# Two more projections formed with seven half products, head norms scaled by ScalarE, and memory attention bridged last, in a two-layer hybrid trunk

## The chip, the cores and the metric

One core of a Trainium2 chip runs the kernel. Its engines are TensorE (matmuls), VectorE, ScalarE, GpSimd and SyncE, each with its own queue of instructions, and 16 DMA engines that move data between the chip's memory and the on-chip buffers. The metric is the device time of one execution, in microseconds (us), as the median of several runs.

## The reference

Two layers over x of shape 256 x 2048 in float32. Every layer makes one wide projection of the normed rows, cuts it into four branches (A sparse attention, B retention, C a gated recurrence, M attention into 256 memory tokens), gates each branch, projects it, weighs it with a sigmoid gate and adds all four. Cut to what matters here:

```python
def hybrid_layer(x, mem, norm_g, w_in, qk_g, ret_g, hgrn_g, lb, w_mem_kv, w_branch, w_out, cos, sin):
    h = rms_norm(x, norm_g)
    u = h @ w_in                                   # 2048 x 15944
    (a_q, a_k, a_v, a_z, a_qi, a_ki, a_wi, b_q, b_k, b_v, b_z,
     c_f, c_i, c_q, c_z, m_q, m_z, gates) = split_cols(u)
    y_a = sparse_index_attention(head_rms_norm(a_q), head_rms_norm(a_k), a_v, a_qi, a_ki, a_wi)
    y_b = head_rms_norm(retention(rope(b_q), rope(b_k) * HEAD_DIM ** -0.5, b_v), ret_g)
    y_c = head_rms_norm(hgrn2(lb + (1.0 - lb) * sigmoid(c_f), c_i, c_q), hgrn_g)
    mkv = mem @ w_mem_kv
    y_m = memory_attention(head_rms_norm(m_q), head_rms_norm(mkv[..., :W]), mkv[..., W:])
    for n, (y, z) in enumerate(((y_a, a_z), (y_b, b_z), (y_c, c_z), (y_m, m_z))):
        merged += sigmoid(gates[:, :, n]) * ((y * silu(z)) @ w_branch[n])
    return x + merged @ w_out
```

## The kernel before

All large products run on TensorE in the type fp32r, with both operands split into a high and a low part: three matmuls (`whi` x high, `wlo` x high, `whi` x low) stand for one. The weights come from memory in slabs of 512 rows and 512 columns (`raw`, 1 MB, four buffers). ScalarE casts a half slab to `whi`, VectorE subtracts to get `wlo` (`cut_piece`), and four pairs of `whi` and `wlo` buffers stand between them and TensorE. A plain slab has two halves, and TensorE runs 12 matmuls of 128x512 on each: two 128-row blocks of weights, times both halves of the 256 rows of x, times three (`gemms`, tiles `u`, `bw`, `wo`).

Some pairs of 512-column chunks are made as a group (`product`, tile `px`): the 256 rows and the 2048 contracted columns are taken as two by two blocks, and seven products of 128 x 1024 by 1024 x 512 stand for eight. The sums of weight blocks that these need are built in four `sum` tiles: a plain DMA from SyncE writes a block into a tile, and DMAs from GpSimd add further blocks (`accum_op`), one for each stage, each after the split that read the tile (`add_block`, `STAGES`). Product number 5 (`RING`) takes plain weights from `raw`. A half of a group's weights feeds only 6 matmuls, since only 128 rows of x (or sums of rows: `r4`, `s1` to `s3`) go with it. Outputs are added up in the tiles `qs`, `us`, `one` (`take`, `combined`). The last sum of the group "c" is made by VectorE from the `raw` tile of product 5 (`sum<-sum,raw`), that of the other groups by one more DMA (`LAST_SUM`). Before, five groups in each layer are done so: the recurrence's values and gate ("c"), and for each of the four branches two of its four gate chunks (`DUO`).

A layer has an early stage (the projections of all branches; the products of group "c" are mingled with plain slabs by `early_tokens`) and a gate stage (gates, four groups, and the bridges, that is branch outputs times `w_branch`, tile `bw`; `gate_tokens`), then the output projection (`wo`). The memory's keys and values for both layers are made first of all and parked in memory.

The program text is written by a planner: after every half of weights, `Stream.pump` lets tasks (Python generators, one for a branch's steps) put their next instructions into the engines' queues, unless a running account of each engine's work says that VectorE or ScalarE is late. `stream.ticks` counts slabs; many tasks wait for a tick (`gates_at + n`), others for a key in `box`. If a task is needed at once and not done, `finish` forces its steps out. The queues then run in the order written. Every instruction is recorded by a helper, so all compute carries line 127 or 145 and is told apart by its tiles.

## Time and profile before

| | before |
|---|---|
| runs | 1814.96, 1815.46, 1817.58 us (median 1815.46) |
| profiled execution | 1814.12 us, of it 1812.3 us from the first to the last instruction |
| TensorE busy | 1803.3 us, 8836 matmuls |
| VectorE, ScalarE, GpSimd busy | 1346.4, 1058.6, 374.4 us |
| moved by DMA | 451.45 MB |
| granted TensorE clock | 1.00 |

In the profile PE is TensorE's matmul, PEld its weight load, DVE is VectorE, ACT ScalarE, POOL GpSimd and SP SyncE. A row of a group gives the tiles written and read, the shapes, the count, the busy time and the mean duration in ns, and behind the bar the idle time of the engine before these instructions with what ended it. Layer 0's early products start at 163 us and its gate stage near 437 us; layer 1's start at 1022 and 1287 us.

### The profile page before, as it was taken

How to read it: one execution, taken by the hardware profiler on the slowest of the kernel's cores; microseconds unless marked ns; L12 is line 12 of the kernel's file. 1: busy time of each engine (PE TensorE's matmuls, PEld its weight loads, DVE VectorE, ACT ScalarE, POOL GpSimd, SP SyncE). 2: the span in 40 equal slices, each digit the busy share in tenths (PEclk: the TensorE clock that was granted, in tenths of full speed). 3: DMA queues.
4: the chain of work that ended last, by engine and by line, in shares of the span. 5: the costliest groups of instructions: out<-in, count | busy, mean ns of one | idle time of the engine just before them, and what ended most of it. 6: DMA issues, size and time to landing. Idle time of an engine off the chain costs nothing.

```text
span 1812.3 us, 24371 instructions
## 1 busy us (share of the span) xinstructions
PE 1803.3 (100%) x8836; PEld 1499.9 (83%) x8836; DVE 1346.4 (74%) x1458; ACT 1058.6 (58%) x1261; POOL 374.4 (21%) x565
## 2 busy tenths in 40 slices
PE   9999999999999999999999999999999999999999
PEld 8889888888888888888887988888888888888887
DVE  5677798786878777687665778878777877777764
ACT  4756565455667656555455656545657765655442
POOL 0022330033232111112131241103333211110200
PEclk9999999999999999999999999999999999999999
DMA  9769965789999999986795996578999999998773
GB/s 332 269 213 289 292 209 180 256 226 277 278 255 278 292 223 274 260 242 219 238 285 155 312 266 207 187 247 225 264 287 272 252 297 228 275 263 234 233 235 136
DMA packets 125321, 451.45 MB, mean 249 GB/s; under 512 B 23184, under 2 KB 45456, under 8 KB 92432
## 3 DMA queue, kind: packets, MB, share of 16 engines
q1 hardware_dynamic: 90480, 357.71, 56.9%
q0 software_dynamic: 34432, 91.92, 26.2%
q8 instruction: 69, 1.13, 0.3%
q14 instruction: 52, 0.43, 0.1%
q10 hardware_dynamic: 288, 0.26, 0.0%
HBM read 419.66 MB, written 6.29 MB: 235 GB/s over the span
## 4 chain that ended last, share of the span: by engine, by line
PE 98%; DVE 1%; DMA 1%; issue 0%; POOL 0%; ACT 0%; SPq 0%; DVEq 0%
PE u L145 50%; PE px L145 21%; PE bw L145 10%; PE wo L145 10%; PE mv L145 2%; PE mk L145 2%; PE ixrp L145 0%; PE mov L145 0%; PE mlg L145 0%; DVE wlo L127 0%; PE bo L145 0%; PE co L145 0%; PE aov L145 0%; DMA xp<-xpi 0%; PE cl L145 0%; PE bs L145 0%
## 5 line engine op out<-in xcount | busy, mean ns | idle before, releaser
L127 DVE TENSOR_TENSOR wlo<-raw,whi 128x1024 fp32r<-128x1024 f32 (+3 forms) x556 | 656.1, 1187 | 344.1 <-ACT whi L127 339.0
L127 ACT CAST whi<-raw 128x1024 fp32r<-128x1024 f32 (+3 forms) x556 | 568.2, 1025 | 581.6 <-PE u L145 352.0
L127 DVE TENSOR_TENSOR wlo<-sum,whi 128x1024 fp32r<-128x1024 f32 x240 | 288.2, 1222 | 67.4 <-ACT whi L127 60.7
L127 ACT CAST whi<-sum 128x1024 fp32r<-128x1024 f32 x240 | 250.2, 1052 | 99.9 <-PE px L145 49.8
L127 POOL DMA_DIRECT2D sum<-in_win x152 | 138.3, 919 | 620.6 <-DVE wlo L127 594.9
L145 PE MATMUL u<-whi,x12h 128*128 128x512 f32 (+2 forms) x176 | 67.4, 383 | 1.5 <-ACT x12h L127 1.5
L145 PE MATMUL u<-whi,x12l 128*128 128x512 f32 (+2 forms) x176 | 67.1, 381 | 0.5 <-DVE x12l L127 0.5
L145 PE MATMUL u<-whi,x13h 128*128 128x512 f32 (+2 forms) x176 | 67.6, 384 | 0.0
L145 PE MATMUL u<-whi,x01h 128*128 128x512 f32 (+2 forms) x176 | 67.5, 383 | 0.0
L145 PE MATMUL u<-whi,x02h 128*128 128x512 f32 (+2 forms) x176 | 67.4, 383 | 0.0
L145 PE MATMUL u<-whi,x11h 128*128 128x512 f32 (+2 forms) x176 | 67.4, 383 | 0.0
L145 PE MATMUL u<-whi,x00h 128*128 128x512 f32 (+2 forms) x176 | 67.3, 383 | 0.0
L145 PE MATMUL u<-whi,x10h 128*128 128x512 f32 (+2 forms) x176 | 67.3, 382 | 0.0
L145 PE MATMUL u<-whi,x03h 128*128 128x512 f32 (+2 forms) x176 | 67.1, 381 | 0.0
L145 PE MATMUL u<-wlo,x12h 128*128 128x512 f32 (+2 forms) x176 | 67.1, 381 | 0.0
L145 PE MATMUL u<-wlo,x13h 128*128 128x512 f32 (+2 forms) x176 | 67.1, 381 | 0.0
L145 PE MATMUL u<-wlo,x11h 128*128 128x512 f32 (+2 forms) x176 | 67.1, 381 | 0.0
L145 PE MATMUL u<-wlo,x01h 128*128 128x512 f32 (+2 forms) x176 | 67.0, 381 | 0.0
L145 PE MATMUL u<-wlo,x02h 128*128 128x512 f32 (+2 forms) x176 | 67.0, 381 | 0.0
L145 PE MATMUL u<-wlo,x10h 128*128 128x512 f32 (+2 forms) x176 | 67.0, 381 | 0.0
L145 PE MATMUL u<-wlo,x00h 128*128 128x512 f32 (+2 forms) x176 | 67.0, 381 | 0.0
L145 PE MATMUL u<-whi,x00l 128*128 128x512 f32 (+2 forms) x176 | 67.0, 381 | 0.0
(496 smaller groups left out, 4482.5 us busy)
## 6 DMA issues: line engine op xcount, KB each, us to landing
raw<-in_win SPq DMA_DIRECT2D x180, 1024.0 KB, 6.7
sum<-in_win POOLq DMA_DIRECT2D x152, 512.0 KB, 8.5
sum<-in_win SPq DMA_DIRECT2D x80, 512.0 KB, 6.9
raw<-in_wbr SPq DMA_DIRECT2D x32, 1024.0 KB, 6.8
raw<-in_wout SPq DMA_DIRECT2D x32, 1024.0 KB, 5.4
raw<-in_wmem SPq DMA_DIRECT2D x12, 1024.0 KB, 4.9
raw<-in_win SPq DMA_DIRECT2D x8, 656.0 KB, 4.3
xc<-in_x SPq DMA_DIRECT2D x8, 512.0 KB, 6.8
```

Of the source, the lines that this page charges most:

```text
L127: return call(*args, **kw)
L145: return self.engine.matmul(out, w, x, **kw)
```

## The change

- Attention's values and gate (`O_AV`, `O_AZ`) become a sixth group "a", behind "c": `EARLY_GROUPS` names the chunks, and the four `sum` tiles go on from "c" to "a" to the gates' groups without being opened anew.
- The chunks of memory attention's and retention's queries and keys (`O_MQ`, `O_MZ`, `O_BQ`, `O_BK`), which stood as plain slabs without products between the early products and the gate stage, are mingled with the products of "c" and "a".
- `scaled_rows`: the multiplication of each head's row by its inverse root (queries, keys, the two branch norms) and of the softmax rows by their inverse sums is done by ScalarE, one instruction for each head and row half, in place of one VectorE instruction.
- Memory attention starts on events (`attended`, `mq`, `mp`) in place of ticks, and the bridges run in the order C, A, B, M in place of C, A, M, B.
- `gate_path` keeps the sigmoid in the tile of its result; the general pool has 23 buffers in place of 22, and the scratch of GpSimd's DMA descriptors 2048 bytes in place of 4096.
- At the end of layer 0 the third chunk's task is stepped twice at once; `finish` lets all other tasks step; the two tables are loaded one at a time.

```diff
-BR_ORDER = (2, 0, 3, 1)
+BR_ORDER = (2, 0, 1, 3)
-GEN, HL, RAW = 22, 4, 4
-DUO, AHEAD, FIRST, MERGED = (2, 0, 3, 1), 10, 0, (0, 3, 2, 1)
-FOLLOWED = dict(zip(DUO, DUO[1:]))
+GEN, HL, RAW = 23, 4, 4
+DUO, AHEAD, FIRST, MERGED = (2, 0, 1, 3), 10, 0, (0, 3, 2, 1)
+FOLLOWED = dict(zip(("c", "a") + DUO, ("a",) + DUO))
-LAST_SUM, RING, EARLY = (True, 1, 0), 5, 8
+LAST_SUM, RING, EARLY, EARLY_GROUPS = (True, 1, 0), 5, 8, {"c": (O_CI, O_CZ), "a": (O_AV, O_AZ)}
...
             elif not moved:
-                ahead = self.tasks[:self.tasks.index(t)]
+                ahead = [u for u in self.tasks if u is not t]
...
 def early_tokens():
-    rows = [("chunk", c, n, b) for c, n in CHUNKS[4:10] for b in range(4)]
-    return rows[:EARLY] + mingled(products_of("c"), rows[EARLY:])
+    rows = [("chunk", c, n, b) for c, n in CHUNKS[4:8] + CHUNKS[10:14] for b in range(4)]
+    return rows[:EARLY] + mingled(products_of("c") + products_of("a"), rows[EARLY:])
...
+    def scaled_rows(out, src, scales, n):
+        for i in range(src.shape[1]):
+            ac.activation(out[:, i, :], src[:, i, :], AF.Copy, scale=scales[:, i:i + 1])
+            if i % n == n - 1 and i < src.shape[1] - 1:
+                yield
...
-            ve.tensor_mul(qn, qn, bc(r, HD))
+            yield from scaled_rows(qn, qn, r, 4)
...
-        ve.tensor_mul(y1, v, bc(r, HD))
+        yield from scaled_rows(y1, v, r, 4)
...
-        ve.tensor_mul(p, p, bc(rc, nk))
+        yield from scaled_rows(p, p, rc, 2)
...
-            ac.activation(sg[:, t, :], ps[:, t, :], AF.Sigmoid, scale=rs[:, t:t + 1])
-            ve.scalar_tensor_tensor(zs[:, t, :], ps[:, t, :], rs[:, t:t + 1], sg[:, t, :],
+            ac.activation(zs[:, t, :], ps[:, t, :], AF.Sigmoid, scale=rs[:, t:t + 1])
+            ve.scalar_tensor_tensor(zs[:, t, :], ps[:, t, :], rs[:, t:t + 1], zs[:, t, :],
...
-        br[0] = stream.add(attend(..., "a", gates_at + 38))
-        box[key("av")] = evac(early_slabs(O_AV), rs, "av")
-        stream.add(keep(key("az"), transposed(gate_path(early_slabs(O_AZ), rs, "az"), "azt")))
+        br[0] = stream.add(attend(..., "a", gates_at + 48, key("attended")))
+        stream.add(keep(key("mq"), put_off(key("attended"), normed_t(early_slabs(O_MQ), rs, qks[:, l, 2:3], "mq"))))
+        stream.add(fetched(f"mk{l}", key("attended")))
+        stream.add(fetched(f"mv{l}", key("mp")))
+        br[3] = stream.add(recall(box, [key("mq"), f"mk{l}", f"mv{l}", key("mz"), key("mp")], "m", gates_at + 115))
...
-        br[1] = stream.add(mixed("bs", "bv", "bz", 0, "b", gates_at + 115))
+        br[1] = stream.add(mixed("bs", "bv", "bz", 0, "b", gates_at + 86))
...
-                    nx[-1].step()
+                    for _ in range(2 if c == 2 else 1):
+                        nx[-1].step()
...
-    nc = bacc.Bacc("TRN2", target_bir_lowering=False, num_devices=1, dynamic_dma_scratch_size=4096)
+    nc = bacc.Bacc("TRN2", target_bir_lowering=False, num_devices=1, dynamic_dma_scratch_size=2048)
```

How the change moves instructions is shown at two places. The first is VectorE's queue in the early stage of layer 0, where product 5 of group "c" is split and the last sum is made from its two `raw` tiles. In it stands before (names with their buffer numbers; the second `raw` tile's split and sum follow behind the last row):

```order
L127 TENSOR_TENSOR wlo_2295<-raw_2008,whi_2294 128x1024
L127 STREAM_TRANSPOSE akpti_2311<-aku_2091 128x1024
L127 TENSOR_TENSOR wlo_2314<-raw_2008,whi_2313 128x1024
L127 TENSOR_TENSOR wlo_2326<-raw_2089,whi_2325 128x1024
L127 TENSOR_TENSOR sum_1270<-sum_1270,raw_2089 128x1024
L127 TENSOR_TENSOR wlo_2337<-raw_2089,whi_2336 128x1024
L127 TENSOR_TENSOR sum_1271<-sum_1271,raw_2089 128x1024
L127 TENSOR_TENSOR us_1910<-us_1910,one_2343 128x512
L127 TENSOR_TENSOR wlo_2359<-raw_2114,whi_2358 128x1024
L127 TENSOR_TENSOR sum_1272<-sum_1272,raw_2114 128x1024
```

Between the first split of the plain slab ahead of product 5 and its second stands one transposition there. The same place of VectorE's queue now:

```order
L127 TENSOR_TENSOR wlo_2129<-raw_1852,whi_2128 128x1024
L127 COPY_PREDICATED cin_2033<-msb_84,cl0_2145 128x32x6
L127 COPY_PREDICATED cin_2033<-msb_84,cl0_2145 128x32x4
L127 COPY_PREDICATED cin_2033<-msb_84,cl0_2145 128x32x2
L127 STREAM_TRANSPOSE aqpti_2181<-aqu_1854 128x1024
L127 TENSOR_TENSOR wlo_2184<-raw_1852,whi_2183 128x1024
L127 TENSOR_TENSOR wlo_2201<-raw_1922,whi_2200 128x1024
L127 TENSOR_TENSOR sum_1271<-sum_1271,raw_1922 128x1024
L127 TENSOR_TENSOR wlo_2212<-raw_1922,whi_2211 128x1024
L127 TENSOR_TENSOR sum_1272<-sum_1272,raw_1922 128x1024
L127 TENSOR_TENSOR us_1881<-us_1881,one_2218 128x512
L127 TENSOR_TENSOR wlo_2235<-raw_1989,whi_2234 128x1024
```

Three predicated copies of the recurrence have moved in ahead of the same run of splits and sums, because product 5 now comes earlier in the stage.

The second place is ScalarE's queue at the turn from layer 0 to layer 1, where the third and the fourth block of layer 1's input are split (`x12h`, `x13h`). Before, TensorE's first matmul with `x12h` reads `whi_8012`, and the queue holds:

```order
L127 CAST whi_8012<-raw_7850 128x1024
L127 CAST whi_8030<-raw_7850 128x1024
L127 CAST whi_8053<-raw_7898 128x1024
L127 CAST whi_8074<-raw_7898 128x1024
L127 ACTIVATE x12h_8085<-xp_7928,ngs_86 128x256 x4
```

Now `x12h` stands further ahead, and it is `x13h` whose first matmul reads `whi_8284`:

```order
L127 CAST whi_8284<-raw_8147 128x1024
L127 CAST whi_8300<-raw_8147 128x1024
L127 CAST whi_8318<-raw_8182 128x1024
L127 CAST whi_8334<-raw_8182 128x1024
L127 ACTIVATE x13h_8340<-xp_8177,ngs_86 128x256 x4
```

In both, the split of the block stands behind the casts of the half that it is first used with and of the three halves after that; what moved is the block, from the third to the fourth.

## The prediction, made before the changed kernel was run

> **What bounds the kernel now.** I read the page's first and fourth part, then the list of waits of TensorE, the chain in order of time, the table by stages, and last the groups and a timeline of the places where the waits are.

> ```profile
> span 1812.3 us, 24371 instructions
> PE 1803.3 (100%) x8836; PEld 1499.9 (83%) x8836; DVE 1346.4 (74%) x1458; ACT 1058.6 (58%) x1261; POOL 374.4 (21%) x565
> PE 98%; DVE 1%; DMA 1%; issue 0%; POOL 0%; ACT 0%; SPq 0%; DVEq 0%
> ```

> TensorE runs from end to end. Its waits, all that the trace has, and three pieces of the chain (start, length, count):

> ```profile
> PE u L145 <- ACT x12h L127: 1.5, 1, 1.5
> PE heat L145 <- DVE warm L127: 1.1, 1, 1.1
> PE px L145 <- DVE wlo L127: 1.0, 1, 1.0
> PE u L145 <- DVE x12l L127: 0.5, 1, 0.5
> PE mk L145 <- ACT whi L127: 0.5, 1, 0.5
> PE mk L145 <- DVE wlo L127: 0.2, 1, 0.2
> 257.93 5.44 PE px L145 x24
> 263.37 5.44 PE u L145 x24
> 861.76 87.05 PE wo L145 x384
> ```

> They sum to 4.8 us in 1812. A run of 24 matmuls of 128x512 takes 5.44 us, and 384 take 87.05, so a matmul's slot is 0.2267 us whether it is a plain one (`u`, `wo`) or a product of a group (`px`). What the change takes from TensorE's list is therefore saved, as long as the weights are split in time. How near the splitting engines are to their limit is seen by stage (length, then busy time of each engine, clock, DMA share and rate):

> ```profile
> 163.00:437.00 274.00, 274.00 (x1534) 224.98 (x1533) 220.07 (x296) 155.37 (x180) 69.53 (x106) 1.00 0.81 243
> 437.00:862.00 425.00, 425.00 (x1920) 353.26 (x1919) 325.60 (x290) 263.46 (x301) 90.38 (x128) 1.00 0.91 259
> 1022.00:1287.00 265.00, 264.90 (x1492) 217.07 (x1491) 218.81 (x295) 150.43 (x175) 66.10 (x102) 1.00 0.78 232
> 1287.00:1721.00 434.00, 433.04 (x1954) 359.53 (x1953) 330.38 (x295) 266.71 (x304) 93.23 (x133) 1.00 0.92 262
> ```

> The columns of busy time are PE, PEld, DVE, ACT, POOL. VectorE has 80 to 83% in the early stages and 76 to 77% in the gate stages.

> [...]

> **The sixth group.** Two chunks as plain slabs are 8 slabs of 24 matmuls, 192; as seven products, each over 8 blocks of 128 rows times three, they are 168. So 24 fewer in a layer, 48 in all: 48 x 0.2267 = 10.9 us off the bound engine.

> The price is on the other engines. Eight slabs are 16 halves to split, 28 halves as products: 24 more halves in two layers. The durations:

> ```profile
> L127 DVE TENSOR_TENSOR wlo<-sum,whi 128x1024 fp32r<-128x1024 f32 x240 | 288.2, 1222 | 67.4 <-ACT whi L127 60.7
> L127 ACT CAST whi<-sum 128x1024 fp32r<-128x1024 f32 x240 | 250.2, 1052 | 99.9 <-PE px L145 49.8
> L127 ACT CAST whi<-raw 128x1024 fp32r<-128x1024 f32 (+3 forms) x556 | 568.2, 1025 | 581.6 <-PE u L145 352.0
> L127 DVE TENSOR_TENSOR qs<-qs,us 128x1024 f32<-128x1024 f32 x10 | 12.2, 1221 | 0.2
> L127 DVE TENSOR_TENSOR mp<-mp,mrc 128x1024 f32<-128x1024 f32 x4 | 4.9, 1224 | 0.1
> L127 ACT ACTIVATE xr<-xr,ngs 128x256 f32<-128x256 f32 x16 | 7.2, 501 | 0.0
> L127 ACT ACTIVATE ap<-alm,anm 128x128 f32<-128x128 f32 x8 | 3.1, 394 | 0.0
> L127 ACT ACT_TABLE_LOAD x14 | 18.0, 1283 | 1.9 <-PEq L1507 1.7
> ```

> VectorE: 24 x 1.22 = 29.3 us, and two groups' sums of outputs (two of 1.22 and two half ones, 3.7 us each) 7.3. The moved norms give back 18 multiplications of 1.22 and two half ones, 23.2. Net +13 us of 1346: no gain overall, but the early stages take all of the splits and few of the savings. There VectorE goes from 220 us in 274 to about 220 + 14.7 + 3.7 - 3.7 = 235 in 268.6, 87%. That is the tightest stage of the kernel from then on.

> ScalarE: 25 us of casts, some 7 of copies, six more table loads (7.7), and the norms as 104 instructions of 128 columns and 24 of 256; by the last rows 104 x 0.39 + 24 x 0.50 = 53. In all +93, to 64% of the span. It lies in the 681 us that ScalarE's casts sat idle for TensorE's buffers (the two rows above; they wait 352.0 and 49.8 for `u` and `px` alone). A step of four scalings is 4 x 0.39 = 1.6 us between two casts, where VectorE had one of 1.22 us. The lead below is 2.8 us, so I cost the norms at nothing; without that cover, 40 such steps would each show some part of 1.6 us.

> [...]

> **Transfers.** In two layers the change drops 12 slabs of 1 MB from SyncE's queue and adds 16 plain and 32 adding `sum` transfers of 0.5 MB.

> ```profile
> raw<-in_win SPq DMA_DIRECT2D x180, 1024.0 KB, 6.7
> sum<-in_win POOLq DMA_DIRECT2D x152, 512.0 KB, 8.5
> sum<-in_win SPq DMA_DIRECT2D x80, 512.0 KB, 6.9
> DMA to landing us min/median/max: 4.3/8.0/13.8
> L127 POOL DMA_DIRECT2D sum<-in_win x152 | 138.3, 919 | 620.6 <-DVE wlo L127 594.9
> ```

> The early stage's 66.6 MB (243 GB/s in 274 us) become 72.9 in 268.6, 271 GB/s. The gate stages move 259 to 262. The rate of products is what the gate stages already have: 14 products among 24 slabs is one in 38 x 5.44 / 14 = 14.8 us, against 28 among 49 there, 15.0. At that rate TensorE waited once for a split in both gate stages, 1.0 us. A `sum` tile's round is issue 0.9, landing 8.0, cast 1.05, split 1.22, or 11.2 us, and fits. GpSimd's queue gets 32 x 0.92 = 29 us more and stays under a quarter busy; the additions stand there among the branches' transposing transfers, as in the gate stages. I cost transfers at nothing. The smaller descriptor scratch adds no instruction; issues 0.9 us apart that land after 8 leave about nine in flight. If half the room were too little, issues would wait for landings, which is the second rival's price.

> **Where the splits come late.** This is VectorE in layer 0, at product 5 of group "c", with the matmul that needs the last split:

> ```profile
> 248.56 1.22 DVE L127 TENSOR_TENSOR wlo<-raw,whi 128x1024 fp32r<-128x1024 f32 x1
> 249.69 1.24 DVE L127 STREAM_TRANSPOSE akpti<-aku 128x1024 f32<-128x1024 f32 x1
> 250.86 2.60 DVE L127 TENSOR_TENSOR wlo<-raw,whi 128x1024 fp32r<-128x1024 f32 x2
> ...
> 260.79 1.22 DVE L127 TENSOR_TENSOR sum<-sum,raw 128x1024 f32<-128x1024 f32 x1
> 261.92 2.35 DVE L127 TENSOR_TENSOR wlo<-raw,whi 128x1024 fp32r<-128x1024 f32 x2
> 252.55 0.39 PE L145 MATMUL u<-wlo,x03h 128*128 128x512 f32 x1
> 263.43 0.39 PE L145 MATMUL u<-wlo,x00h 128*128 128x512 f32 x1
> L127 DVE COPY_PREDICATED cin<-msb,cl 128x192 f32<-128x192 uint8 x4 | 1.6, 411 | 3.2 <-PE cl L145 3.2
> ```

> The first split ends at 249.78, 2.8 us ahead of its matmul at 252.55. The four halves of product 5 feed TensorE for 5.44 us, but with their sums they hold VectorE for about 9, and the lead at the next slab is 263.43 - 263.14 = 0.3 us. Now three predicated copies stand in the same run. The row gives 0.41 us for the largest, so with two smaller ones about 1.0: 0.3 - 1.0 = -0.7, a wait of 0.7 us in layer 0. In layer 1 four short multiplications replace the transposition, a draw. And the run starts with less lead than 2.8 us, for products come every 14.8 us in place of some 18. The bounds a layer are nothing (a longer lead at the start) and 0.7 + 2.8 = 3.5 us (no lead left). I take 1.0, near the lower end, because in the gate stages, with products as close, the one wait for a split was 1.0 us in two stages: 2.0 in all, bounds 0 and 7. Behind the late split stand VectorE's other branch work and ScalarE's casts, which catch up in the next plain slab (5.44 us against 2.4 of splits).

> **Moves at nothing.** The turn to layer 1: `x12h`'s wait of 1.5 and 0.5 us goes, since its task is stepped earlier. But `x13h` is now the one forced out behind the casts of the three halves after, so the same 2.0 us stands at the fourth block; 0 net, bounds -2 and +1. Bridges in another order are as many matmuls as before, and no bridge (`bw`) is in the list of waits; the cover is the ticks that each branch is ahead, and without it a bridge would wait for one landing, about 8 us. The reused sigmoid tile and the 23rd buffer change no count. The wait of 1.0 us at `px` may go as retention and memory trade places: -1 to 0, I take 0.

> **The sum**, against the profiled execution's own 1814.1 us (span 1812.3 and 1.8 around it): -10.9 + 2.0 = 1805.2. The median of the runs lies 1.4 above that execution, so on its scale 1806.6.

> **Rivals.**
> First, no new wait: VectorE's lead holds at product 5. Then 1815.5 - 10.9 = 1804.6, and 1803.6 with the old `px` wait gone. For it: the lead recovers in every slab. Against: 0.3 us is all that was left at this place, with more work now.
> Second, slower: the early stage's transfers are too many. Its place is the `sum` tiles; it decides when landing grows from 8 to past 11.6 us, for then the round exceeds 14.8. At 13.8, the longest seen, each round lacks 2.2 us; 12 such products a layer are 24 x 2.2 = 53 us, less part that the lead takes: about 1840 at worst and 1820 with 0.65 us each (-10.9 + 15.6). Against it: 0.91 of DMA share in the gate stages goes without waits.
> Third, ScalarE late: the two steps of a scaling follow closely and hold the casts for 3.2 us, 0.4 past the lead of 2.8. Over 20 scalings that is 8 us, with the late splits 10, so 1815.5 - 10.9 + 10 = 1814.6, no change. It decides where two steps stand between neighbouring casts. Against: the 681 idle us. [...]
> Fourth, the change does not save what it says: were TensorE's slots stretched by something else that feeds it, fewer matmuls would leave 1815.5. The equal slots speak against it. [...]

> **Numbers.** Forecast 0.70, first rival 0.15, second 0.06, third 0.06, fourth 0.03. Predicted 1806.6 us. The range reaches from 1803.0 (first rival with half a microsecond) to 1812.0, the upper bound of 7 us at the late splits (1811.6) and a little of the third. A measurement of this kernel tells 0.2%, 3.6 us, from no change. Faster: forecast and first rival nearly whole and a part of the third, 0.89; same 0.06; slower 0.05.

> **What would show it.** Right: about 48 fewer matmuls and a PE busy time near 1792; VectorE near 1360, ScalarE near 1150; a wait of PE for `wlo` near 240 us and near 1080, a microsecond each; `x13h` in place of `x12h`; landings of `sum` near 8. Wrong: waits of ScalarE for `sum` transfers that reach TensorE in the early stages, a wait at `bw`, or casts behind scalings of a norm with TensorE idle.

## The result, and the profile after

The changed kernel takes 1826.05 us (median of 6 runs, 1822.79 to 1827.5), beside 1815.21 us (1812.65 to 1817.58, 6 runs) of the kernel before: ratio 1.0063, 95% interval 1.0052 to 1.0073. It is slower, by 0.6%, and the interval lies clear of 1. The forecast was 1806.6.

Its page has 48 matmuls fewer, as the change says, and the chain is no longer TensorE alone:

```profile
span 1824.2 us, 24581 instructions
PE 1802.5 (99%) x8788; PEld 1492.5 (82%) x8788; DVE 1353.7 (74%) x1470; ACT 1131.3 (62%) x1431; POOL 405.2 (22%) x597
PE 85%; DMA 7%; DVE 4%; issue 2%; ACT 2%; SPq 0%; POOL 0%; DVEq 0%; ACTq 0%; POOLq 0%
```

The list of TensorE's waits (us in total, times, longest) shows where it went. It sums to 17.6 us, 4.8 before:

```profile
PE px L145 <- DVE wlo L127: 6.3, 4, 4.3
PE px L145 <- ACT whi L127: 3.1, 3, 1.4
PE u L145 <- DVE wlo L127: 1.9, 5, 0.4
PE u L145 <- ACT x13h L127: 1.5, 1, 1.5
PE mov L145 <- DVE mpl L127: 1.4, 1, 1.4
```

Most of the first two rows is two places. **Stall A** (3.9 us of waits) is in layer 0 at 182 to 192 us, at product 1 of group "c", which reads `sum` tiles. The chain in order of time, of after and then of before (start, length, what):

```profile
168.94 18.48 DMA sum<-in_win
...
187.52 1.05 ACT whi L127
...
188.60 1.24 DVE wlo L127
...
189.88 2.50 PE px L145 x5
```

```profile
171.35 2.75 PE px L145 x12
174.09 5.44 PE u L145 x24
179.53 2.75 PE px L145 x12
182.28 5.44 PE u L145 x24
```

An adding transfer takes 18.5 us to land, where the page's median is 8.2; cast and split follow it, and TensorE follows them. In before a slab (`u` x24, 5.44 us) stood between any two halves of a product there. In after the halves of product 1 stand next to each other: its first half ends in the first row here, and the second, which begins in the next, already has to wait (TensorE's timeline; in brackets the idle time and what ended it):

```profile
182.18 0.40 PE L145 MATMUL px<-whi,s3l 128*128 128x512 f32 x1
183.86 0.50 PE L145 MATMUL px<-whi,s3h 128*128 128x512 f32 x1 [1.28 <-ACT whi L127]
```

**Stall B** (4.3 us) is in layer 1. The timeline (start, length; in brackets what ended the idle time before it):

```profile
1351.26 1.22 DVE L127 TENSOR_TENSOR bs0s<-bs,table 128x1024 f32<-128x1024 f32 x1 [9.64 <-DMA table<-in_cf]
1352.40 1.22 DVE L127 TENSOR_TENSOR wlo<-sum,whi 128x1024 fp32r<-128x1024 f32 x1
1353.53 1.22 DVE L127 TENSOR_TENSOR wlo<-raw,whi 128x1024 fp32r<-128x1024 f32 x1
1353.67 0.80 PE L145 MATMUL px<-wlo,x13h 128*128 128x512 f32 x1 [4.28 <-DVE wlo L127]
```

Retention's first multiplication reads the decays table, which is now requested only when the rotated keys are in the box. The load is issued at 1342.3 us. VectorE's queue stands for 9.64 us, with two weight splits behind it, and TensorE runs out of split weights.

Behind each stall the granted clock is 0.50 in place of 1.00 for 6.83 us. The table of stretches of 3.41 us (busy time of PE, PEld, DVE, ACT, POOL; then the granted clock, the DMA share and GB/s), first around stall A, then around stall B:

```profile
182.24:185.65 3.41, 1.37 (x5) 0.67 (x4) 1.23 (x1) 1.04 (x1) 0.00 (x0) 1.00 1.03 303
185.65:189.06 3.41, 2.00 (x5) 0.95 (x4) 0.46 (x1) 1.54 (x2) 0.00 (x0) 0.50 0.95 333
189.06:192.48 3.42, 2.95 (x7) 2.12 (x7) 3.42 (x4) 2.41 (x4) 0.00 (x0) 0.50 0.52 161
...
1349.60:1353.01 3.41, 0.00 (x0) 0.00 (x0) 1.75 (x2) 0.45 (x1) 0.00 (x0) 1.00 0.04 16
1353.01:1356.42 3.41, 2.75 (x8) 2.27 (x9) 1.74 (x2) 2.70 (x4) 0.00 (x0) 0.50 0.42 132
1356.42:1359.84 3.42, 3.42 (x13) 2.94 (x13) 1.85 (x2) 1.32 (x2) 0.00 (x0) 0.50 0.07 26
```

In the run `e10_ring_layer0` below, a stretch that is busy throughout holds 8 matmuls at half clock and 16 in the next one at full clock (the last fence of this text), so I count half of TensorE's busy time at half clock as lost. In stall A it is busy 4.95 us of two such stretches, so 2.5 us are lost; in stall B 6.17 us, so 3.1. Against the profiled execution before, then: -10.9 (48 matmuls), +12.8 (waits, 17.6 - 4.8), +5.6 (clock), 7.5 in all. The spans differ by 11.9. Of the 4.4 left, some 2 us lie at the listed waits themselves: the list counts from the end of a matmul's row, 0.39 us after its start, while the slot is 0.2267 us, so each of the 20 waits (6 before) costs 0.16 us more than it says. The starts of the two traces show besides 14 more gaps of 0.1 to 0.4 us over the slot between matmuls of 512 columns, 1.7 us together, which the list leaves out.

### The profile page after: what moved, and what is told of

Read it like the earlier page. It is cut to its first block, busy times and chain, and to the rows that moved or that the text cites. A ratio compares the mean times of both kernels' runs of the same rounds, so it can differ in the third digit from the quotient of the medians.

```text
span 1824.2 us, 24581 instructions
## 1 busy us (share of the span) xinstructions
PE 1802.5 (99%) x8788; PEld 1492.5 (82%) x8788; DVE 1353.7 (74%) x1470; ACT 1131.3 (62%) x1431; POOL 405.2 (22%) x597
## 4 chain that ended last, share of the span: by engine, by line
PE 85%; DMA 7%; DVE 4%; issue 2%; ACT 2%; SPq 0%; POOL 0%; DVEq 0%; ACTq 0%; POOLq 0%
PE u L145 38%; PE px L145 20%; PE bw L145 10%; PE wo L145 10%; DMA sum<-in_win 4%; DVE wlo L127 3%; PE mv L145 2%; PE mk L145 2%; ACT whi L127 1%; DMA raw<-in_win 1%; DMA azt<-azti 1%; DMA table<-in_cf 0%; DVE sum L127 0%; DMA cnpt<-cnpti 0%; DMA apT<-apT0i 0%
## 5 line engine op out<-in xcount | busy, mean ns | idle before, releaser
L127 DVE TENSOR_TENSOR wlo<-raw,whi 128x1024 fp32r<-128x1024 f32 (+3 forms) x532 | 626.2, 1185 | 335.0 <-ACT whi L127 327.4
L127 ACT CAST whi<-raw 128x1024 fp32r<-128x1024 f32 (+3 forms) x532 | 542.6, 1023 | 498.5 <-PE u L145 286.9
L127 DVE TENSOR_TENSOR wlo<-sum,whi 128x1024 fp32r<-128x1024 f32 x288 | 344.3, 1219 | 77.2 <-ACT whi L127 67.7
L127 ACT CAST whi<-sum 128x1024 fp32r<-128x1024 f32 x288 | 298.8, 1051 | 101.2 <-PE px L145 57.5
L127 POOL DMA_DIRECT2D sum<-in_win x184 | 169.1, 923 | 860.0 <-DVE wlo L127 787.8
L127 POOL DMA_DIRECT2D mgp<-mgpi x64 | 34.1, 540 | 138.9 <-DVE mgpi L127 123.7
L145 PE MATMUL u<-whi,x13h 128*128 128x512 f32 (+2 forms) x160 | 61.6, 385 | 1.5 <-ACT x13h L127 1.5
L145 PE MATMUL u<-wlo,x01h 128*128 128x512 f32 (+2 forms) x160 | 61.2, 382 | 0.8 <-DVE wlo L127 0.8
L145 PE MATMUL u<-wlo,x11h 128*128 128x512 f32 (+2 forms) x160 | 61.0, 381 | 0.8 <-DVE wlo L127 0.8
L145 PE MATMUL u<-whi,x13l 128*128 128x512 f32 (+2 forms) x160 | 61.2, 382 | 0.5 <-DVE x13l L127 0.5
L145 PE MATMUL u<-whi,x02h 128*128 128x512 f32 (+2 forms) x160 | 61.4, 384 | 0.0
L145 PE MATMUL u<-wlo,x02h 128*128 128x512 f32 (+2 forms) x160 | 61.0, 381 | 0.3 <-DVE wlo L127 0.3
L145 PE MATMUL u<-wlo,x13h 128*128 128x512 f32 (+2 forms) x160 | 61.3, 383 | 0.0
L145 PE MATMUL u<-whi,x12h 128*128 128x512 f32 (+2 forms) x160 | 61.2, 382 | 0.0
L145 PE MATMUL u<-wlo,x12h 128*128 128x512 f32 (+2 forms) x160 | 60.9, 381 | 0.1
L145 PE MATMUL u<-whi,x03h 128*128 128x512 f32 (+2 forms) x160 | 61.0, 381 | 0.0
L145 PE MATMUL u<-whi,x11h 128*128 128x512 f32 (+2 forms) x160 | 60.9, 381 | 0.0
L145 PE MATMUL u<-whi,x10h 128*128 128x512 f32 (+2 forms) x160 | 60.9, 381 | 0.0
L145 PE MATMUL u<-whi,x00h 128*128 128x512 f32 (+2 forms) x160 | 60.9, 381 | 0.0
L145 PE MATMUL u<-whi,x01h 128*128 128x512 f32 (+2 forms) x160 | 60.9, 381 | 0.0
L145 PE MATMUL u<-whi,x02l 128*128 128x512 f32 (+2 forms) x160 | 60.8, 380 | 0.0
L145 PE MATMUL u<-wlo,x03h 128*128 128x512 f32 (+2 forms) x160 | 60.8, 380 | 0.0
## 6 DMA issues: line engine op xcount, KB each, us to landing
raw<-in_win SPq DMA_DIRECT2D x168, 1024.0 KB, 6.9
sum<-in_win POOLq DMA_DIRECT2D x184, 512.0 KB, 8.2
sum<-in_win SPq DMA_DIRECT2D x96, 512.0 KB, 6.5
raw<-in_wbr SPq DMA_DIRECT2D x32, 1024.0 KB, 6.6
raw<-in_wout SPq DMA_DIRECT2D x32, 1024.0 KB, 5.6
raw<-in_wmem SPq DMA_DIRECT2D x12, 1024.0 KB, 5.5
xc<-in_x SPq DMA_DIRECT2D x8, 512.0 KB, 7.3
```

The costliest lines, as they stand in the source:

```text
L127: return call(*args, **kw)
L145: return self.engine.matmul(out, w, x, **kw)
```

## Experiments

Each run was timed beside the kernel before on the same chip. Waits are the sum of TensorE's list, "half" the time at clock 0.5 (without the last 3 us of a program, when TensorE is done), both from the profiled execution.

| run | median us | ratio to before, 95% | waits | half |
|---|---|---|---|---|
| before | 1815.21 | | 4.8 | 0 |
| after | 1826.05 | 1.0063 [1.0052, 1.0073] | 17.6 | 13.7 |
| e1_table_early | 1835.22 | 1.0114 [1.0100, 1.0128] | 22.5 | 27.3 |
| e2_keynorm_vector | 1823.37 | 1.0051 [1.0038, 1.0063] | 14.6 | 10.2 |
| e3_slab_between | 1828.45 | 1.0079 [1.0066, 1.0092] | 21.0 | 13.7 |
| b1_scratch_2048 | 1814.64 | 0.9999 [0.9990, 1.0008] | 5.9 | 0 |
| e4_rest | 1821.55 | 1.0045 [1.0033, 1.0058] | 16.3 | 6.8 |
| e5_rest_slab0 | 1818.58 | 1.0024 [1.0014, 1.0034] | 14.4 | 6.8 |
| e6_all_vector | 1837.72 | 1.0126 [1.0111, 1.0142] | 26.5 | 23.9 |
| e7_rest_slab0_keys | 1816.48 | 1.0009 [1.0000, 1.0017] | 11.5 | 3.4 |
| e8_wait_a | 1821.68 | 1.0040 [1.0026, 1.0054] | 8.7 | 10.2 |
| e8_wait_b | 1824.47 | 1.0057 [1.0044, 1.0069] | 11.6 | 13.7 |
| e9_late_c_2 | 1813.32 | 0.9995 [0.9986, 1.0004] | 8.4 | 3.4 |
| e9_late_c_6 | 1824.11 | 1.0056 [1.0043, 1.0068] | 18.2 | 13.7 |
| e10_ring_both | 1814.05 | 0.9997 [0.9988, 1.0006] | 11.2 | 3.4 |
| e10_ring_layer0 | 1812.34 | 0.9984 [0.9975, 0.9993] | 8.9 | 3.4 |
| e10_ring_layer1 | 1814.58 | 1.0001 [0.9993, 1.0010] | 12.4 | 3.4 |

**Stall A: the order or the norm?** Two candidates stood: the two-step norm of the memory keys by ScalarE, which pushes the first `sum` transfers about 2 us later, and the halves of product 1 next to each other.

```diff
 # e2: memory keys alone
-            yield from scaled_rows(qn, qn, r, 4)
+            if rs is None:
+                ve.tensor_mul(qn, qn, r[:, :, None].to_broadcast([128, 8, HD]))
+            else:
+                yield from scaled_rows(qn, qn, r, 4)
 # e3: spaces of the early groups, both layers
+BETWEEN_EARLY = (4, 4, 4, 4, 3, 2, 2)
```

> The changed kernel with the norm of the memory keys alone, at the start of the program, by one VectorE multiply again instead of eight ScalarE scalings in two steps. Theory (a): the two-step norm is what puts the parked keys' writes and the first sum transfers some 3 us later on the full queues at 150 to 185 us; then ScalarE's waits for the sum tiles at 173 to 187 us shrink to those of the kernel before (13 us in the layer, none above 2 us), the half-clock stretch at 185 us goes, and the time is 1818 to 1820 us. Theory (b): the dense order of the first group's two parts is the cause; then 1825 to 1827 us and the same half-clock stretch at about 185 us.

> The changed kernel with a projection slab of 5.4 us again between the two parts of product 1 of the early groups, as before (the spaces 4, 4, 4, 4, 3, 2, 2 for the early groups instead of 4, 3, 4, 4, 3, 2, 3). Theory (b), the dense order is the cause of the stall at 178 to 192 us: its waits and the half-clock stretch at 185 us go, 1818 to 1820 us. Theory (a), the two-step norm of the memory keys is the cause: 1825 to 1827 us, the stall is there again, moved by some us. If either alone is enough to bridge the 3 us, both this run and the one with the keys' norm on VectorE give 1818 to 1820 us.

ScalarE's and TensorE's waits at 172 to 194 us, in the run with the keys' norm on VectorE, and in the run with the slab between:

```profile
ACT whi L127 <- DMA sum<-in_win: 9.2, 3, 3.7
PE px L145 <- ACT whi L127: 2.1, 1, 2.1
PE px L145 <- DVE wlo L127: 1.2, 2, 0.7
```

```profile
ACT whi L127 <- DMA sum<-in_win: 7.8, 3, 3.7
PE px L145 <- DVE wlo L127: 0.3, 1, 0.3
```

The first kept the stall and its 6.8 us at half clock, though its four transfers land when those of before did (170.9 to 185.1 us there, 170.3 to 184.6 before, 173.3 to 187.4 after). The second lost the stall, though its transfers land as late as those of after (172.8 to 186.9). So the order is the cause of this stall. It needs the slow landings too, for in after the same two halves adjoin at two more places. In group "a" of layer 0, at 295.5 us, the adding transfers land in 9.2 us at most (DMA share 0.90 from 265 to 300 us) and TensorE does not wait. In group "c" of layer 1, at 1042 us, they take up to 13.4 us (share 1.03 from 1010 to 1045 us), ScalarE waits up to 3.8 us for a `sum` and TensorE 1.2.

The 2.7 us that the first run gained by the medians do not show what the norm costs: its wait in stall B was 3.6 us in place of 4.3, with one window at half clock in place of two. Neither total came as a theory had it, for the run with the slab was slower than after: layer 1 came into another order, and there VectorE now stood 12.9 us at the table.

```profile
DVE bs0s L127 <- DMA table<-in_cf: 12.9, 1, 12.9
PE u L145 <- DVE wlo L127: 8.1, 1, 8.1
```

**Stall B: load early, or wait elsewhere?** An early load is the obvious cure, so it came first; then the load as late as in the change, but a rest of three ticks before the use, so that other work passes.

```diff
 # e1
-stream.add(table(0, lambda: key("bk") in box))
+stream.add(table(0, lambda: stream.ticks >= gates_at - 10))
 # e4, in retain(), behind "while not decays.done"
+            yield from stream.rest(3)
```

> The changed kernel with one trigger moved: the decays table is loaded ten ticks before the gate products begin, not when the rotated retention keys are in the box. Everything else stands as it was. Theory (late transfers): the 9.6 us idle of VectorE at the table in layer 1 goes, and with it TensorE's 4 us wait behind it and the half-clock stretch of 6.8 us at 1353 us; about 8.5 us of the 1826.1 us go, so 1817 to 1819 us, and the clock near 1353 us is 1.0. Rival (ScalarE's norms and the denser product groups make the splits late everywhere, the two stalls are only where it shows): less than 3 us go, 1823 us or more. Rival (the smaller descriptor scratch slows the transfers of POOL): no change, 1826 us.

> The changed kernel with a rest of three ticks between the landing of the decays table and retention's first multiply; the table is still loaded when the rotated keys are in the box, so the buffers are handed out as in the changed kernel up to there. Theory (the table's 9 us landing blocks VectorE's queue in layer 1, and an earlier load pays for it with a buffer): the 9.6 us idle of VectorE at the table goes or shrinks below 3 us, no half-clock stretch near 1353 us, no new wait on folded tiles; 1817 to 1820 us. Rival (the denser layer-1 product stream is late on its own there, the table only hides it): another wait of 3 us or more stands at 1335 to 1360 us, and the time stays at 1823 us or more.

Neither theory had the first result: 9 us slower. VectorE waits for no table, but a copy on ScalarE now waits (timeline of that run):

```profile
1340.32 0.59 ACT L127 COPY one<-px 128x512 f32<-128x512 f32 x1 [9.07 <-DMA raw<-in_win]
1340.94 0.69 DVE L127 TENSOR_TENSOR us<-us,one 128x512 f32<-128x512 f32 x1 [8.25 <-ACT one L127]
1340.96 0.79 PE L145 MATMUL px<-whi,x12h 128*128 128x512 f32 x1 [8.01 <-ACT one L127]
```

`one` reads a finished `px` tile, which TensorE's matmuls write; nothing that it needs is being loaded. In the trace this copy waits on 14 counters of transfers. They are the 14 on which the 16 transfers of one fold count, issued from 1322.7 to 1332.9 us (a fold finishes a transposition by moving strips of a tile, here from `bkpti` to `bkpt`). Its last transfer landed at 1339.84, 0.5 us before the copy. So `one` is given the buffer of `bkpti`, the fold's source, and waits until that is read. "raw" in the row is only a transfer that landed about then. That it came to this buffer because the early table holds one of the 23 general buffers for longer is likely, but no run here shows it by itself. With the rest instead (e4), the table's wait and the half-clock stretch behind it are gone, and 4.5 us are won, 1.5 us short of the forecast. What took its place is again a buffer, in this list of the run e7 below, with the same first row as e4:

```profile
DVE cnl L127 <- PE aov L145: 8.5, 1, 8.5
PE u L145 <- DVE wlo L127: 2.3, 1, 2.3
```

`cnl` (the low part of the c branch's folded product, a general buffer too) is made from `cnpt` and `cnh`, and `aov`, attention's last product, makes neither. So I read the wait as one for a buffer that `aov` still read.

**Both cures, and the keys.** The slab only in layer 0, with the rest; then the keys' norm on VectorE besides.

```diff
-    ... mingled(products_of("c") + products_of("a"), rows[EARLY:])
+    ... mingled(products_of("c") + products_of("a"), rows[EARLY:], BETWEEN_EARLY if l == 0 else BETWEEN_PRODUCTS)
```

> Both cures in one: the rest of three ticks behind the decays table, and the slab between the two parts of product 1 in the early groups of layer 0 alone (layer 1 keeps the spaces of the changed kernel). Theory (two late transfers with a half-clock stretch behind each carry the loss): stall at 180 to 192 us gone (it was 7.2 us over the slots, 0.6 in the run with the slab), the one at 1342 to 1360 us gone or under 2 us, clock 1.0 throughout: 1809 to 1813 us, faster than the kernel before. Rival (each cure moves the order and the buffers, and another tile is late in its place): one new half-clock stretch or wait of over 3 us, 1815 to 1824 us.

> The run with the rest and the slab in layer 0, and the memory keys' norm on VectorE besides. Theory: the keys' norm gave 2 us of the 11 by itself, at the start of the program; with the slab in place it gives 0 to 2 us more, 1808 to 1812 us. Rival (the order that results decides, not the edit): it differs from the run without it by 3 us or more in either direction, with a stall at a place that neither edit touches.

7.5 and 9.6 us come off the changed kernel's time, which was 10.8 above the kernel before. So the two stalls carry most of that, as the theory has it; but its 1809 to 1813 us were missed by 6 us, to the rival's side, and the 1808 to 1812 of the second run by 4.5. One window at half clock stands in each, behind the wait for `cnl`'s buffer, and e5 has another at 1597 us, behind ScalarE's wait of 5.9 us for the memory's values (`mvhi`).

**The rivals of the prediction.** The smaller scratch alone in the kernel before, and every norm back on VectorE in the changed one:

```diff
 # b1
-dynamic_dma_scratch_size=4096
+dynamic_dma_scratch_size=2048
 # e6
     def scaled_rows(out, src, scales, n):
-        for i in range(src.shape[1]): ...
+        ve.tensor_mul(out, src, scales[:, :, None].to_broadcast(...))
```

> The kernel before with one number changed: the scratch for descriptors of dynamic transfers is 2048 instead of 4096. Theory (late transfers by the order of the work): no change, 1814.0 to 1816.5 us, ratio 0.999 to 1.001. Rival (the smaller scratch holds back POOL's accumulating transfers): 3 us or more are lost, 1818 us or more, and the four adds of 160 to 172 us land later than in the kernel before (170.3 to 184.6 us there).

> The changed kernel with every norm and softmax scaling by one VectorE multiply again, none by ScalarE; the sixth group, the bridges and the tables stand as in the changed kernel. Rival (ScalarE's 160 scalings delay the casts and make the splits late): the small late splits at 254, 301, 473, 1110 and 1331 us (some 0.5 us each) go and the time falls to 1820 us or less. Theory (order and late transfers): the stalls at about 185 and 1350 us stand, possibly moved, and the time is 1823 to 1829 us.

The smaller scratch cost nothing by the medians (ratio 0.9999), though the four adds land 0.8 to 0.9 us later (171.1 to 185.6 us). Without ScalarE's scalings the kernel is 11.7 us slower still, so they are not what makes the changed kernel slow. What they cost by themselves this run does not show, since its two largest stalls, at 491 and at 1303 us, are the table again, now in layer 0, and a tile `cny` that waits for the end of a fold (its counters are those of the fold of `bqpti`):

```profile
DVE bs0s L127 <- DMA table<-in_cf: 9.4, 1, 9.4
...
DVE cny L127 <- DMA bqpt<-bqpti: 11.1, 1, 11.1
PE u L145 <- DVE wlo L127: 9.3, 1, 9.3
```

**The price of one wait.** In the kernel before, dummy VectorE work at one place of the last layer, 8 or 12 additions:

```diff
             def take(ps):
+                for _ in range(8 if l == L - 1 and c == 0 else 0):
+                    nc.vector.tensor_add(idle, idle, idle)
```

> The kernel before with eight dummy VectorE additions (0.69 us each, 5.5 us together) ahead of the first output addition of the last layer's last product stage, and nothing else: one wait of known place. From the lead of the splits there, some 3 us, TensorE should idle some 2 to 3 us. Theory (a wait that leaves a 3.4 us window more than half idle is followed by windows at half clock): the span grows by the wait alone if no window gets over half idle, by the wait and 1.7 us if one does: 2 to 5 us. Rival (the half-clock stretches have another cause, the crowded transfers): the wait alone, and the clock stays at 1.0.

> The same with twelve dummy additions (8.3 us together): TensorE idles some 5 to 6 us, 2.8 us more than with eight. Theory (windows): at least one window of 3.4 us is over half idle, the clock shows one to three windows at half, and the loss is the wait and 1.7 us for each: 7 to 11 us over the kernel before. Rival (transfers): 5 to 6 us, clock 1.0.

The forced wait was 3.9 and 6.8 us, larger than the 2 to 3 and 5 to 6 expected. By the medians the runs lost 7.2 and 10.0 us, the first more than its 2 to 5, the second within its 7 to 11. Stretches of 3.41 us from the one in which the wait begins, of the run with 8 and of the run with 12:

```profile
1764.23:1767.64 3.41, 1.33 (x6) 0.75 (x4) 3.24 (x6) 1.04 (x1) 0.00 (x0) 1.00 0.65 269
1767.64:1771.05 3.41, 1.55 (x4) 1.29 (x5) 3.41 (x5) 0.00 (x0) 0.00 (x0) 0.50 0.41 153
1771.05:1774.47 3.42, 3.42 (x10) 2.65 (x9) 1.76 (x3) 0.00 (x0) 0.00 (x0) 0.50 0.48 104
1774.47:1777.88 3.41, 3.41 (x17) 2.80 (x16) 1.23 (x1) 1.35 (x2) 0.00 (x0) 1.00 0.98 345
```

```profile
1764.64:1768.05 3.41, 0.77 (x4) 0.31 (x2) 3.24 (x6) 1.04 (x1) 0.00 (x0) 1.00 0.51 214
1768.05:1771.46 3.41, 0.00 (x0) 0.00 (x0) 3.31 (x6) 0.00 (x0) 0.00 (x0) 0.50 0.00 0
1771.46:1774.88 3.42, 2.62 (x6) 2.15 (x7) 3.42 (x5) 0.00 (x0) 0.00 (x0) 0.50 0.41 153
1774.88:1778.29 3.41, 3.41 (x9) 2.64 (x8) 0.69 (x2) 0.54 (x1) 0.00 (x0) 0.50 0.83 197
```

The spans grew by 7.4 and 10.7 us, more than the waits, while the transfers had a share of 0.00 to 0.65 up to the second half-clock window: in both runs half clock came behind TensorE's idle time and without crowded transfers. (In before the clock stays at 1.00 with a share of 1.03 over 35 us; the row is in the next section.) Wait plus half of what runs at half clock is 3.9 + 4.97/2 = 6.4 and 6.8 + 6.03/2 = 9.8. Both runs have another such stretch of 3.41 us at 962 us, behind the 2 us that TensorE waits at the turn from layer 0 to layer 1 (1.7 us lost); with it 8.1 and 11.5, 0.7 and 0.8 above what was measured.

**A version that beats both?** In layer 1 the split of the c branch's folded product two or six ticks later, on top of e7; then, on the first of these, one slab moved from behind product 6 to product 5, where VectorE makes the last sums.

```diff
 # e9 (2 or 6)
-gates_at + 18)
+gates_at + 18 + 2 * l)
 # e10, in both layers, layer 0 or layer 1
+(4, 4, 4, 4, 2, 4, 1)
```

> The run with rest, slab and keys' norm, and the split of the c branch's folded product two ticks later in layer 1. There that split's low half waited 8.5 us on VectorE for a buffer that attention's last product still read, with two weight splits of a product behind it (2.3 us wait of TensorE and a half-clock window, 5.7 us over the slots at 1340 to 1360 us). Theory (the 23 general buffers couple the branches): with the split behind those two, the 5.7 us go to under 1.5 us: 1811 to 1813 us, faster than the kernel before by 2 to 3 us. Rival (any move puts another tile on a buffer just in use): 1814 to 1820 us with a new wait elsewhere in layer 1.

> The same with six ticks instead of two: the split then comes behind the whole block of softmax and retention work, and its buffer has been free for long. Theory: as with two ticks or better, 1810 to 1813 us. Rival: the c branch's first gate products now wait for the split, 3 us or more, 1815 us or more.

> The run with rest, keys' norm and the split of c two ticks later, and in the early groups of both layers one slab taken from behind product 6 to product 5 (spaces 4, 4, 4, 4, 2, 4, 1), where VectorE makes the last sums between the weight splits. Theory (VectorE's queue at product 5 is short by the sums, the forecast's plus 2 us): the late splits at 245 to 248, 347, 1104 and 1325 us (0.5 to 1.3 us each, some 3.5 us together) go: 1809 to 1811 us. Rival (the order shifts which buffer a tile gets): a new wait of over 2 us, 1814 us or more.

> The same in layer 0 alone; layer 1 keeps the changed kernel's spaces. Theory: the late splits at 245 to 248 and 347 us go, 1.3 us each: 1810.5 to 1812.5 us. Rival: a new wait, 1814 us or more.

> The same in layer 1 alone; layer 0 keeps the slab between the parts of product 1 and two slabs behind product 6. Theory: the late splits at 1104 and 1325 us go, 0.5 us each: 1812 to 1813.5 us. Rival: layer 1 is the one where buffers were just in use, so here a new wait stands, 1815 us or more.

Two ticks took the stall behind `cnl` away, 3.2 us by the medians, which makes the kernel level with the one before, not 2 to 3 us faster. With six the bridge itself was late (`PE bw` waits 6.5 us for `cnh`). The slab at product 5 in layer 0 removed the late splits at 245 to 248 us, but not the one at 346, where rotations of q stand in VectorE's queue. That is the best run, 1812.34 us, inside what was expected, though one of the two splits that were to go has stayed. Its interval ends just under 1, it is the best of 15 runs, and 0.16% is less than the 0.2% that the prediction called telling. In layer 1 the same edit gave new gaps near 1203 and 1294 us (2.5 and 1.9 us over the slot), and in both layers together they cancelled the gain. The rival blamed buffers for this, but the traces show the order: at 1203 us sums of outputs and the rotations of q stand in VectorE's queue ahead of a weight split, and at 1294 us ScalarE's queue stands 3.6 us for the fold to `cnpt`, with casts behind it. The best run is 1.1 us ahead of the kernel before by the two profiled spans (2.6 by the medians), not 10.9, for it pays 4.1 us of waits more, 1.7 of clock and, as the remainder, 4.0 of short gaps.

## Why the prediction was wrong

On the scale of the profiled executions the forecast was 1805.2 us and the changed kernel took 1825.95, so 20.8 us were missed. By the lists and tables above, 8.2 of them are waits in the two stalls (3.9 in A, 4.3 in B), 5.6 are the clock behind them, 2.6 are other waits beyond the 2.0 forecast, and 4.4 are what the list of waits does not count.

**48 matmuls, -10.9 us:** right, and all of it is in the count. PE's busy time did not fall to 1792, because a half-clock stretch counts as busy (5.6 us), and so do the short gaps inside a matmul's row of 0.39 us (4.4). VectorE's and ScalarE's times were 1354 and 1131 us, forecast near 1360 and 1150.

**Late splits, +2.0:** right in kind, and in part by luck in size. Outside the two stalls the list of after has 2.7 us of waits for `wlo` (6.3 + 1.9, less 4.3 in stall B and 1.2 in stall A). Right behind product 5 of group "c" stand only two of them, 0.4 us each, at 254 and 1110 us, where a microsecond each was forecast. Three more of 0.4 are at 301, 474 and 1331 us, and 0.8 at 1046 us belong to the transfers. In the runs with the slab in layer 0 the wait at product 5 is larger (245 to 248 us), and it vanishes with another slab there. Not foreseen was that the recurrence's small steps (at 301 us) and rotations of q (at 346 us in the later runs) come into the same queue.

**The turn at nothing:** right. `x13h` took over `x12h`'s 1.5 us, `x13l` the 0.5.

**Transfers at nothing: the step that failed first.** I compared a tile's round (11.2 us) with the mean distance of products (14.8). The loss is at the nearest pair, the adjoining halves of product 1, and in the stretch with the longest landings, 18.5 us (in e2 13.8 were enough). The new order of products has the first. The trace of before had a sign of the second in two rows that the prediction does not use: a DMA share (next to last column) of 1.03 at 150 to 185 us, and ScalarE already waiting 2.7 us for a `sum` at 172 to 194 us, covered by the slab between.

```profile
150.00:185.00 35.00, 35.00 (x185) 31.16 (x184) 23.79 (x27) 21.75 (x26) 7.48 (x12) 1.00 1.03 321
```

```profile
ACT whi L127 <- DMA sum<-in_win: 2.7, 1, 2.7
```

The second rival named the mechanism, put a price on the mean and gave it 0.06. The expected 271 GB/s were 257, and the page's median landing stayed at 8: no mean would have told.

**Moves at nothing: the step that failed next.** My text on moves has the turn and the bridges, but not the decays table's new trigger, though the list of changes says that the two tables are loaded one at a time. Before, layer 1's table was requested at 1175 us and first read at 1316; now it is requested at 1342 and wanted at once, a load of 8 us, by VectorE, in whose queue the weight splits stand. A wait was to be priced by what is queued behind it: two splits, 4.3 us of TensorE, and 3.1 of clock.

**No term for the clock.** Every wait was priced at its own length. 13.7 us at half clock cost 5.6 us, and every run with the sixth group shows some.

**ScalarE late (third rival):** not borne out. Neither stall stands behind scalings, and with all of them back on VectorE the kernel is 11.7 us slower; how much of that the scalings themselves save stays open.

**The 23rd buffer "changes no count":** true, and beside the point. What a buffer changes is who waits for whom: `one`, `cnl` and `cny` each waited 8 to 11 us for a buffer's last reader, in runs whose edits were elsewhere. In e1, e4, e5 and e7 that is what took a cured stall's place. In e3 it was the table, requested at a worse moment. The new order of the bridges, the sigmoid's tile and the edits of `finish` were not run alone, so what each moved stays open.

## What to carry to other kernels

Price a new stream of transfers at the closest pair of its uses in the stretch with the slowest landings (here 18.5 us, where the median is 8.2), not at its mean rate. Look up, for every load whose trigger moves, who stands behind its first user in that engine's queue; and add to a wait of TensorE what the clock behind it may take: here some 2.5 us behind the 3.9 of stall A, 3.1 behind the 4.3 of stall B, and behind the 2 us at the turn 1.7 in e8_wait_a and nothing in the changed kernel. In a kernel whose buffers are all in use, an edit hands other buffers to later tiles, so a cure is measured together with the order it brings, not alone.

## What of the hardware was not expected

```profile
984.40:987.81 3.41, 1.96 (x9) 1.30 (x7) 1.56 (x2) 1.75 (x4) 0.00 (x0) 1.00 0.40 144
987.81:991.23 3.42, 2.81 (x11) 2.04 (x12) 2.80 (x7) 2.47 (x8) 0.40 (x1) 1.00 0.39 140
```

```profile
979.65:983.06 3.41, 1.35 (x6) 0.49 (x4) 1.93 (x4) 2.77 (x6) 0.00 (x0) 1.00 0.03 13
983.06:986.47 3.41, 3.41 (x8) 2.76 (x9) 1.45 (x5) 1.11 (x4) 0.71 (x1) 0.51 0.48 154
986.47:989.89 3.42, 3.42 (x16) 2.73 (x16) 0.69 (x1) 1.43 (x3) 0.00 (x0) 0.99 0.00 0
```

So a wait of 2 us was enough for a window at half clock. Back to full clock it took one window busy throughout or nearly so: 2.95 us at stall A was enough, while windows with 2.62 us (e8_wait_b) and 2.75 (stall B) were followed by another at half.
